# Transposing the gated FFN values on VectorE instead of TensorE in three of the four FFNs of a two-layer decoder trunk

## The chip, the cores and the metric

The kernel runs on one core of one Trainium2 chip. The metric is the device time of one execution in microseconds (us): the median of three runs was 1585.8 us, and they lay between 1585.21 and 1585.86. One more execution was recorded by the hardware profiler; its time was 1585.53 us and its span (from the first recorded instruction to the last) 1583.4 us. All rows below come from that one.

The engines are named as in the profile: PE is TensorE's matmul, PEld its loading of stationary operands, DVE is VectorE, ACT is ScalarE, POOL is GpSimd, and SP is SyncE, which issues the weight transfers.

## The reference

Two layers over 256 tokens of width 1024. Each layer adds to the running state `h`, in this order: half of a first FFN, the sum of four gated token mixers, a cross attention on a memory of 256 rows, and half of a second FFN. So there are four FFNs in all. One of them is

```python
def swiglu(x, w_gate, w_up, w_down):
    return (jax.nn.silu(x @ w_gate) * (x @ w_up)) @ w_down

h = h + 0.5 * swiglu(rms_norm(h, ffn1_norm[l]), ffn1_w_gate[l], ffn1_w_up[l], ffn1_w_down[l])
```

with `w_gate` and `w_up` of 1024 x 2816 and `w_down` of 2816 x 1024, all float32.

## The kernel before, in words

**Tiling.** The tokens are two blocks (`b`) of 128. Every large matrix product goes through `linear`: the stationary operand is a 128 x 128 piece of the transposed activations, the moving operand 512 columns of weights, and the result has the tokens on partitions. Float32 is imitated by three products of two-part numbers: each operand is a high part and a low part, and high x high, low x high and high x low are summed in PSUM. So one 128-deep step of one token block is three matmuls of 128x512.

**Weights.** `plan` lists all weights in the order of use, in chunks of 128 x 2048 (four 128-deep steps of 512 columns, 1 MB). `fetch` issues the transfer of a chunk on SP's queue into `wr`, and for each half of it ACT copies the high part into `wh` (L350) and DVE subtracts to get the low part `wl` (L351). There are three buffers each of `wr`, `wh` and `wl`. A chunk feeds 24 matmuls: 12 for each token block, in the order high x high, low x high, high x low, so that `wl` is needed last.

**An FFN.** The 2816 hidden columns are 11 groups of 256. A group's moving operand holds 256 gate columns beside 256 up columns, so a group is two chunks (the depth is 1024) and 48 matmuls; groups 0 and 1 go together, their chunks taken in turn. When a token block of a group is complete, `evac` runs ACT's Silu on the gate half (L557) and DVE multiplies it with the up half (L558) into `toks`, tokens on partitions. The second product needs the hidden columns on partitions, so `hidden` turns them: four 128 x 128 transposes on PE (L547) into a PSUM bank `ht`, and then `split` makes the two parts of it in the tile `hid`, the high one by ACT (L364) and the low one by DVE (L365). All 11 `hid` tiles live until the second product has read them: two halves of 512 output columns, each 22 steps deep in six chunks (the last of them half a chunk).

**Order of the work.** PE's instructions run in the order in which the program writes them. The other engines' streams are put in order by a planner, which goes by the program's order and by estimated durations; on the chip every engine then runs its own stream strictly in order. Small chains of work are Python generators: a chain advances at a `tick`, and `yield n` means not before n steps later; a step is one token block of one chunk, 12 matmuls. `hidden` begins with `yield 2`, so PE's four transposes of a group stand one whole chunk after the group's end.

**Pools.** The tag `toks` has three buffers of 128 x 512; the tag `gate` has four, and outside the FFNs holds gates of the mixers and values of the cross attention. In the first FFN of the first layer DVE also builds the attention bias tables (L642, L644).

Of the kernel before, what the change touches and what calls it, by code (L numbers as in the profile page):

```python
# [19 lines left out]
P = 128  # L20
# [3 lines left out]
NB = S // P  # L24
KD = D // P
DFF = 2816
KF = DFF // P
# [125 lines left out]
def program(tc, a, out, upto="all"):  # L153
    nc = tc.nc
    act, dve, pool, pe = nc.scalar, nc.vector, nc.gpsimd, nc.tensor
# [20 lines left out]
    def bank(name):  # L176
        return aux.tile([P, 512], F32, tag="aux", name=name)

    def m4(name, dtype=F32):
        return mp.tile([P, 1024], dtype, tag="m", name=name)  # L180
# [7 lines left out]
    def f2(name, tag="f", bufs=5):  # L188
        return fp.tile([P, 512], F32, tag=tag, name=name, bufs=bufs)
# [9 lines left out]
    ident = cp.tile([P, P], F32, tag="ident", name="ident")  # L199
# [21 lines left out]
    def pcol(l, name, i=0, n=1):  # L221
        o = l * NPC + PO[name][0] + i
        return pcs[:, o:o + n]
# [18 lines left out]
    def advance(c):  # L242
        try:
            c[1] = next(c[0])
            c[2] = now
        except StopIteration:
            chains.remove(c)
# [6 lines left out]
    def start(gen):  # L254
        c = [gen, 0, now]
        chains.append(c)
        advance(c)
        return c

    def begin():  # L260
        nonlocal now
        now += 1

    def tick():
        for c in list(chains):
            if c in chains and ready(c):
                advance(c)

    def finish(c):
        while c in chains:  # L270
            assert isinstance(c[1], int) or all(e in events for e in c[1]), c[1]
            advance(c)
# [12 lines left out]
    def plan():  # L285
# [16 lines left out]
        for l in range(L):  # L302
            yield from ffn(l, "1")
            yield from chunks([win[l, G_QK], win[l, G_RV]], KD, 512)
            yield from chunks([win[l, G_RG]], KD, 512)
            yield from chunks([a["wmisc"][l]], KD, MISC)
            for g in (G_X0, G_X1):
                yield from chunks([win[l, g]], KD, 512, HELD)
            yield from chunks([win[l, G_Z]], KD, 512)
            yield from branch(l, 0)  # L310
            yield a["wmla"][l], 1536, 0
            for g in (G_DQ, G_DK):
                yield from chunks([win[l, g]], KD, 512, HELD)
            yield from chunks([win[l, G_DV]], KD, 512)
            for i in range(1, 4):
                yield from branch(l, i)
            yield from chunks([a["w_out"][l, c] for c in range(2)], KD, 512)
            for n in ("xa_wk", "xa_wq", "xa_wv"):
                for c in range(2):
                    yield from chunks([a[n][l, c]], KD, 512, 0 if n == "xa_wv" else HELD)  # L320
            yield from chunks([a["xa_wo"][l, c] for c in range(2)], KD, 512)
            yield from ffn(l, "2")
# [31 lines left out]
    def weights(n):  # L354
        for _ in range(AHEAD - len(fetched)):
            fetch()
        hi, lo, m = fetched.pop(0)
        assert m == n
        return hi, lo


    def split(hi, lo, src):

        act.activation(hi, src, AF.Copy)  # L364
        dve.tensor_tensor(lo, src, hi.bitcast(F32), ALU.subtract)  # L365

    def linear(kt, n, xT, evacs):

        ps = [[lin.tile([P, 512], F32, tag="lin", name="lin") for _ in range(NB)] for _ in evacs]
        per = 2048 // n  # L370
        for k0 in range(0, kt, per):
            m = min(per, kt - k0)
            for p_, evac in zip(ps, evacs):
                hi, lo = weights(m * n)
                if now < 4:

                    begin()
                    for k in range(m):
                        for b in range(NB):
                            for part, w in ((0, hi), (1, hi), (0, lo)):  # L380
                                pe.matmul(p_[b][:, :n], lhsT=xT(part, k)[:, b * P:(b + 1) * P],  # L381
                                          rhs=w[:, k * n:(k + 1) * n], start=k == 0 and w is hi and part == 0, stop=False)
                    tick()
                    begin()
                    tick()
                    continue
                for b in range(NB):
                    begin()
                    for part, w in ((0, hi), (1, hi), (0, lo)):
                        for k in range(m):  # L390
                            first = k0 + k == 0 and w is hi and part == 0
                            last = k0 + k == kt - 1 and w is lo
                            pe.matmul(p_[b][:, :n], lhsT=xT(part, k0 + k)[:, b * P:(b + 1) * P],  # L393
                                      rhs=w[:, k * n:(k + 1) * n], start=first, stop=last)
                    if k0 + m == kt:
                        evac(b, p_[b][:, :n])
                    tick()
# [33 lines left out]
    def blk(b):  # L431
        return slice(b * P, (b + 1) * P)
# [91 lines left out]
    def norm(l, name):  # L524
        return Transposed(hh, pcol(l, name, 0, 8), "r" + name)

    def add_to_h(c, factor, nxt, wait=1):
        def evac(b, ps):
            nonlocal paced
            if factor == 1.0:  # L530
                paced = dve.tensor_tensor(h[b][c], ps, h[b][c], ALU.add)  # L531
            else:
                paced = dve.scalar_tensor_tensor(h[b][c], ps, factor, h[b][c], ALU.mult, ALU.add)
            if nxt is not None and b == NB - 1:
                nxt.begin(c, wait)
        return evac

    def ffn(xT, nxt):
        hid = {}

        def hidden(g, toks):
            yield 2
            t4 = m4("hid", F32R).rearrange("p (s f t) -> p s f t", s=2, f=2)
            ps = bank("ht").rearrange("p (f t) -> p f t", f=2)
            for b in range(NB):
                for k in range(2):
                    pe.transpose(ps[:, k, blk(b)], toks[:, b, k * P:(k + 1) * P], ident)  # L547
            split(t4[:, 0], t4[:, 1], ps)
            hid[g] = t4

        def group(g):
            toks = f2("toks", "toks", 3).rearrange("p (b t) -> p b t", b=2)

            def evac(b, ps):
                nonlocal paced
                sg = fp.tile([P, 256], F32, tag="sg", name="sg")
                act.activation(sg, ps[:, :256], AF.Silu, scale=xT.r[:, b:b + 1])  # L557
                paced = dve.scalar_tensor_tensor(toks[:, b], ps[:, 256:], xT.r[:, b:b + 1], sg, ALU.mult, ALU.mult)  # L558
                if b == NB - 1:
                    start(hidden(g, toks))  # L560

            return evac

        linear(KD, 512, xT, [group(0), group(1)])
        for g in range(2, 11):
            linear(KD, 512, xT, [group(g)])
        for c in range(2):
            linear(KF, 512, lambda part, k: hid[k // 2][:, part, k % 2, :], [add_to_h(c, 0.5, nxt, 1 if c else 5)])


    def tables():
# [671 lines left out]
    x = Given(hh, pcol(0, "ffn1", 0, 8), "rffn1")  # L1243
# [12 lines left out]
    made = start(tables())  # L1256
    for l in range(L):
        n = norm(l, "mix")
        ffn(x, n)
        if stages == 1:  # L1260
            break
        x = norm(l, "xa")
        mem, m = mixers(l, n, x)
        if stages == 2:
            break
        n = norm(l, "ffn2")
        cross(l, mem, m, x, n)
        if stages == 3:
            break
        x = norm(l + 1, "ffn1") if l + 1 < L else None  # L1270
        if x is None:
            fn = bias.rearrange("p h k -> p (h k)")[:, :D]
            act.dma_start(fn, a["fnorm"])
        ffn(n, x)
        if stages == 4:
            break
# [17 lines left out]
```

## Time and profile before

| | us |
|---|---|
| median of three runs | 1585.8 |
| profiled execution, its own time | 1585.53 |
| its span | 1583.4 |
| PE busy | 1572.2 |
| PEld busy | 1345.1 |
| DVE busy | 1065.2 |
| ACT busy | 830.2 |
| POOL busy | 26.0 |

Busy times are sums over the span. PE's matmuls are pipelined and their ends are modelled, so a duration of one matmul is longer than the distance from its start to the next one's; what a run of matmuls takes is read from the chain in order of time. In the chain (the work that ended last, followed back from the end) a line has the start, the length and the number of instructions. Where two DVE instructions stand as one line of the timeline, the length runs from the first's start to the last's end.

### The profile page before, as it was taken

The numbers are of one execution on the slowest core, as the hardware profiler recorded it, in microseconds if no ns is written. First come the engines' busy times: TensorE is split into PE (matmuls) and PEld (weight loads), VectorE is DVE, ScalarE is ACT, GpSimd is POOL, SyncE is SP. The second block draws the span as 40 slices with busy tenths as digits, with TensorE's granted clock in tenths as the row PEclk, the third lists the DMA queues.
The fourth block names the chain that finished last, engine by engine and source line by source line (L and its number), as shares of the span: only waits on it lengthen the run. The fifth ranks groups of instructions, "written<-read, shape, count | busy, mean of one in ns | idle before, by whom it ended". The sixth has DMA issues, their size and how long they took to land.

```text
span 1583.4 us, 20797 instructions
## 1 busy us (share of the span) xinstructions
PE 1572.2 (99%) x8208; PEld 1345.1 (85%) x8208; DVE 1065.2 (67%) x1704; ACT 830.2 (52%) x1236; POOL 26.0 (2%) x40
## 2 busy tenths in 40 slices
PE   9999999999999999999999999999999999999998
PEld 7888889898888988888888888898988899888886
DVE  5887699997787656554565546697656766565543
ACT  6744446566655545444454444475575555554443
POOL 0000000000000000000000000000000000000000
PEclk9999999999999999999999999999999999999999
DMA  7655544444655444555555556444546554455552
GB/s 291 239 180 179 194 169 160 165 164 144 212 214 177 169 160 163 187 182 182 191 188 188 183 176 209 151 159 157 184 149 237 186 186 164 156 182 176 191 174 74
DMA packets 43153, 284.73 MB, mean 180 GB/s; under 512 B 4784, under 2 KB 5168, under 8 KB 11056
## 3 DMA queue, kind: packets, MB, share of 16 engines
q1 hardware_dynamic: 40464, 276.12, 51.3%
q10 hardware_dynamic: 2592, 7.29, 1.4%
q8 instruction: 64, 1.05, 0.3%
q14 instruction: 33, 0.27, 0.0%
HBM read 282.34 MB, written 1.05 MB: 179 GB/s over the span
## 4 chain that ended last, share of the span: by engine, by line
PE 98%; DMA 1%; ACT 0%; DVE 0%; issue 0%; POOLq 0%; POOL 0%; ACTq 0%
PE lin L393 77%; PE lin L411 11%; PE tr L422 2%; PE ht L547 1%; PE xo L1191 1%; PE lin L381 1%; PE xs L1145 1%; DMA bcs<-bcols 1%; PE up L953 1%; PE my L869 0%; PE ds L1038 0%; PE ms L989 0%; PE pt L680 0%; DMA pcs<-pcols 0%; ACT wh L350 0%
## 5 line engine op out<-in xcount | busy, mean ns | idle before, releaser
L351 DVE TENSOR_TENSOR wl<-wr,wh 128x1024 fp32r<-128x1024 f32 (+3 forms) x536 | 624.7, 1191 | 375.1 <-ACT wh L350 372.7
L350 ACT ACTIVATE wh<-wr 128x1024 fp32r<-128x1024 f32 (+3 forms) x536 | 533.2, 1030 | 493.4 <-PE lin L393 381.7
L393 PE MATMUL lin<-wh,xh 128*128 128x512 f32 (+1 forms) x1200 | 328.5, 395 | 1.1 <-ACT wh L350 0.9
L393 PE MATMUL lin<-wl,xh 128*128 128x512 f32 (+1 forms) x1200 | 320.7, 389 | 0.6 <-DVE wl L351 0.6
L393 PE MATMUL lin<-wh,xl 128*128 128x512 f32 (+1 forms) x1200 | 320.4, 389 | 0.0
L393 PEld LDWEIGHTS lin<-wl,xh 128*128 128x128 f32 x1200 | 225.1, 188 | 48.0 <-DVE wl L351 1.4
L393 PEld LDWEIGHTS lin<-wh,xl 128*128 128x128 f32 x1200 | 225.3, 188 | 47.0
L393 PEld LDWEIGHTS lin<-wh,xh 128*128 128x128 f32 x1200 | 219.2, 188 | 43.7 <-ACT wh L350 2.2
L393 PE MATMUL lin<-wh,hid 128*128 128x512 f32 x704 | 176.0, 390 | 0.0
L393 PEld LDWEIGHTS lin<-wh,hid 128*128 128x128 f32 x704 | 131.6, 188 | 27.1
L393 PE MATMUL lin<-wl,hid 128*128 128x512 f32 x352 | 95.4, 389 | 0.0
L393 PEld LDWEIGHTS lin<-wl,hid 128*128 128x128 f32 x352 | 66.1, 188 | 13.9
L557 ACT ACTIVATE sg<-lin,rffn 128x256 f32<-128x256 f32 x88 | 40.9, 464 | 65.0 <-PE lin L393 63.7
L644 DVE SCALAR_TENSOR_TENSOR bias<-ge,d,bias 128x384 f32<-128x384 f32 x124 | 69.4, 610 | 0.3
L411 PE MATMUL lin<-xh,wh 128*128 128x256 f32 x384 | 62.0, 283 | 0.0
L558 DVE SCALAR_TENSOR_TENSOR toks<-lin,rffn,sg 128x256 f32<-128x256 f32 x88 | 42.3, 480 | 27.7 <-ACT sg L557 27.6
L411 PE MATMUL lin<-xh,wl 128*128 128x256 f32 x384 | 60.5, 279 | 0.0
L411 PE MATMUL lin<-xl,wh 128*128 128x256 f32 x384 | 60.5, 279 | 0.0
L411 PEld LDWEIGHTS lin<-xh,wh 128*128 128x128 f32 x384 | 52.0, 188 | 0.3
L411 PEld LDWEIGHTS lin<-xl,wh 128*128 128x128 f32 x384 | 51.7, 188 | 0.0
L411 PEld LDWEIGHTS lin<-xh,wl 128*128 128x128 f32 x384 | 51.7, 188 | 0.0
L444 ACT ACTIVATE junk<-h 128x512 bf16<-128x512 f32 x36 | 22.4, 623 | 30.6 <-DVE h L531 16.9
(395 smaller groups left out, 1559.4 us busy)
## 6 DMA issues: line engine op xcount, KB each, us to landing
wr<-gu SPq DMA_DIRECT2D x86, 1024.0 KB, 5.1
wr<-win SPq DMA_DIRECT2D x68, 1024.0 KB, 5.1
wr<-dn SPq DMA_DIRECT2D x40, 1024.0 KB, 4.9
wr<-wbr SPq DMA_DIRECT2D x16, 1024.0 KB, 4.9
wr<-w_out SPq DMA_DIRECT2D x8, 1024.0 KB, 5.2
wr<-xa_wk SPq DMA_DIRECT2D x8, 1024.0 KB, 4.9
wr<-xa_wq SPq DMA_DIRECT2D x8, 1024.0 KB, 4.9
wr<-xa_wv SPq DMA_DIRECT2D x8, 1024.0 KB, 5.0
```

Source lines behind the costliest of these rows:

```text
L350: last = act.activation(hi[:, s], r[:, s], AF.Copy)
L351: dve.tensor_tensor(lo[:, s], r[:, s], hi[:, s].bitcast(F32), ALU.subtract)
L381: pe.matmul(p_[b][:, :n], lhsT=xT(part, k)[:, b * P:(b + 1) * P], rhs=w[:, k * n:(k + 1) * n], start=k == 0 and w is hi and part == 0, sto ...
L393: pe.matmul(p_[b][:, :n], lhsT=xT(part, k0 + k)[:, b * P:(b + 1) * P], rhs=w[:, k * n:(k + 1) * n], start=first, stop=last)
L411: pe.matmul(ps[i][:, j * 256:(j + 1) * 256], lhsT=ws[w][:, o:o + P], rhs=xT(part, k0 + k), start=k0 + k + part + w + j == 0, stop=k0 + k = ...
L422: pe.transpose(ps[:, k * P:(k + 1) * P], src[:, k * P:(k + 1) * P], ident)
L444: act.activation(j[:, :src.free_size()], src, AF.Square, accum_out=out_)
L547: pe.transpose(ps[:, k, blk(b)], toks[:, b, k * P:(k + 1) * P], ident)
L557: act.activation(sg, ps[:, :256], AF.Silu, scale=xT.r[:, b:b + 1])
L558: paced = dve.scalar_tensor_tensor(toks[:, b], ps[:, 256:], xT.r[:, b:b + 1], sg, ALU.mult, ALU.mult)
L644: dve.scalar_tensor_tensor(bias[:, hd], ge, d8[:, hd, i + 1:i + 2], bias[:, hd], ALU.mult, ALU.add)
L953: pe.matmul(ps[:, :n], lhsT=lowT[p_][:, k0 + k, blk(b)], rhs=wm[w][:, o + k * n:o + (k + 1) * n], start=i == 0, stop=i == len(seq) - 1)
```

## The change

In all FFNs but the very first (`busy`), the PE transposes and their PSUM bank are gone. DVE transposes the same values from `toks` in SBUF into a tile `turned` in SBUF, with the tag `gate`. DVE's transpose turns blocks of 32 x 32. Each of the 16 instructions of a group takes one quarter of the partitions (32 tokens of each block) and four blocks of 32 hidden columns, 128 values for each of the 32 partitions, and writes them to the quarter of the partitions that these columns belong to. They go out in four batches of four, at four successive steps, and after the fourth comes the same `split`, which now reads SBUF. The second product asks for a group's tile through `hT`, which first drives a chain to its end if it has not come there yet.

```diff
-    def ffn(xT, nxt):
-        hid = {}
+    def ffn(xT, nxt, busy=False):
+        hid, started = {}, {}
 
         def hidden(g, toks):
-            yield 2
             t4 = m4("hid", F32R).rearrange("p (s f t) -> p s f t", s=2, f=2)
-            ps = bank("ht").rearrange("p (f t) -> p f t", f=2)
-            for b in range(NB):
-                for k in range(2):
-                    pe.transpose(ps[:, k, blk(b)], toks[:, b, k * P:(k + 1) * P], ident)
-            split(t4[:, 0], t4[:, 1], ps)
+            if busy:
+                yield 2
+                ps = bank("ht").rearrange("p (f t) -> p f t", f=2)
+                for b in range(NB):
+                    for k in range(2):
+                        pe.transpose(ps[:, k, blk(b)], toks[:, b, k * P:(k + 1) * P], ident)
+                split(t4[:, 0], t4[:, 1], ps)
+            else:
+
+                t = f2("turned", "gate", 4)
+                src = toks.rearrange("p b (k j a) -> p k b j a", k=2, j=4)
+                dst = t.rearrange("p (k b i a) -> p k b i a", k=2, b=2, i=4)
+                for i in range(4):
+                    for j in range(4):
+                        dve.transpose(dst[j * 32:(j + 1) * 32, :, :, i], src[i * 32:(i + 1) * 32, :, :, j])
+                    yield 1
+                split(t4[:, 0], t4[:, 1], t.rearrange("p (k t) -> p k t", k=2))
             hid[g] = t4
...
-                    start(hidden(g, toks))
+                    started[g] = start(hidden(g, toks))
...
+        def hT(part, k):
+            if k // 2 not in hid:
+                finish(started[k // 2])
+            return hid[k // 2][:, part, k % 2, :]
+
         for c in range(2):
-            linear(KF, 512, lambda part, k: hid[k // 2][:, part, k % 2, :], [add_to_h(c, 0.5, nxt, 1 if c else 5)])
+            linear(KF, 512, hT, [add_to_h(c, 0.5, nxt, 1 if c else 5)])
...
-        ffn(x, n)
+        ffn(x, n, l == 0)
```

The call for the second FFN of a layer, `ffn(n, x)`, is unchanged and so takes the new way in both layers.

## Rows read from the trace of the kernel before

**Rows 1.** The profile's page: busy time of each engine with its share of the span and its instructions, and the chain that ended last by engine and by line.

```profile
PE 1572.2 (99%) x8208; PEld 1345.1 (85%) x8208; DVE 1065.2 (67%) x1704; ACT 830.2 (52%) x1236; POOL 26.0 (2%) x40
...
PE 98%; DMA 1%; ACT 0%; DVE 0%; issue 0%; POOLq 0%; POOL 0%; ACTq 0%
```

**Rows 2.** The chain that ended last, in order of time, over the last FFN: start, length, what.

```profile
1418.71 0.44 PE ht L547 x4
1419.15 10.93 PE lin L393 x48
1430.08 0.44 PE ht L547 x4
1430.52 10.93 PE lin L393 x48
...
1509.65 0.44 PE ht L547 x4
1510.08 10.93 PE lin L393 x48
1521.01 0.44 PE ht L547 x4
1521.45 54.46 PE lin L393 x240
```

**Rows 3.** The same view in the second FFN of the first layer: the first and the last of nine neighbouring groups, and the second product behind them.

```profile
635.03 10.93 PE lin L393 x48
645.96 0.44 PE ht L547 x4
646.39 10.93 PE lin L393 x48
...
725.96 10.93 PE lin L393 x48
736.89 0.44 PE ht L547 x4
737.33 38.13 PE lin L393 x168
```

**Rows 4.** Busy time of each engine by stretch (ten groups of that FFN, and its second product), with the number of instructions; then the granted clock as a share of full speed, the DMA engines' busy share, and GB/s.

```profile
core 0: us, PE busy (x) PEld busy (x) DVE busy (x) ACT busy (x) POOL busy (x), PEclk, DMA share, GB/s
...
635.00:748.70 113.70, 113.70 (x520) 94.02 (x519) 61.26 (x69) 52.43 (x69) 0.00 (x0) 1.00 0.55 181
748.70:805.00 56.30, 56.30 (x258) 46.73 (x257) 31.26 (x37) 25.65 (x34) 1.07 (x1) 1.00 0.59 196
```

**Rows 5.** DVE's instructions in order of time over one group of that FFN; in brackets DVE's idle time before them and what ended it.

```profile
646.18 2.36 DVE L351 TENSOR_TENSOR wl<-wr,wh 128x1024 fp32r<-128x1024 f32 x2 [2.69 <-ACT wh L350]
648.45 0.68 DVE L365 TENSOR_TENSOR hid<-ht,hid 128x512 fp32r<-128x512 f32 x1
649.71 0.48 DVE L558 SCALAR_TENSOR_TENSOR toks<-lin,rffn,sg 128x256 f32<-128x256 f32 x1 [0.57 <-ACT sg L557]
652.10 1.23 DVE L351 TENSOR_TENSOR wl<-wr,wh 128x1024 fp32r<-128x1024 f32 x1 [1.91 <-ACT wh L350]
653.25 0.48 DVE L558 SCALAR_TENSOR_TENSOR toks<-lin,rffn,sg 128x256 f32<-128x256 f32 x1
653.64 1.22 DVE L351 TENSOR_TENSOR wl<-wr,wh 128x1024 fp32r<-128x1024 f32 x1
657.54 2.36 DVE L351 TENSOR_TENSOR wl<-wr,wh 128x1024 fp32r<-128x1024 f32 x2 [2.69 <-ACT wh L350]
```

**Rows 6.** DVE's rows by line and shape, over the whole span: count, busy time, mean ns of one, and its idle time before them.

```profile
L742 DVE TENSOR_SCALAR yr<-ro,mv,gnr 128x128 f32<-128x128 f32 x16 | 5.5, 404 | 4.6 <-POOL gnr L739 4.6
...
L632 DVE COPY bias<-cst 128x128 f32<-128x128 f32 x4 | 0.9, 219 | 3.8 <-DMA cst<-consts 3.8
...
L657 DVE TENSOR_TENSOR qc<-rp,rp 128x128 f32<-128x128 f32 x4 | 1.1, 285 | 0.0
...
L1050 DVE SCALAR_TENSOR_TENSOR dsb<-dsb,r 128x128 f32<-128x128 f32 x8 | 2.4, 346 | 0.0
...
L655 DVE TENSOR_TENSOR rp<-lin,tabr 128x256 f32<-128x256 f32 x4 | 1.7, 415 | 0.0
...
L558 DVE SCALAR_TENSOR_TENSOR toks<-lin,rffn,sg 128x256 f32<-128x256 f32 x88 | 42.3, 480 | 27.7 <-ACT sg L557 27.6
```

**Rows 7.** PE's matmuls in order of time at the start of a chunk, the second of the next group.

```profile
657.51 1.18 PE L393 MATMUL lin<-wh,xh 128*128 128x512 f32 x4
658.53 1.08 PE L393 MATMUL lin<-wh,xl 128*128 128x512 f32 x4
659.45 0.85 PE L393 MATMUL lin<-wl,xh 128*128 128x512 f32 x3
```

**Rows 8.** Who waited for whom from 635 to 748 us: total, times, the longest.

```profile
DVE wl L351 <- ACT wh L350: 46.9, 20, 3.0
ACT wh L350 <- PE lin L393: 46.5, 20, 3.4
ACT sg L557 <- PE lin L393: 14.6, 9, 1.6
DVE toks L558 <- ACT sg L557: 5.1, 9, 0.6
```

**Rows 9.** ACT's instructions in order of time over the same group.

```profile
645.08 2.01 ACT L350 ACTIVATE wh<-wr 128x1024 fp32r<-128x1024 f32 x2 [3.07 <-PE lin L393]
647.00 0.58 ACT L364 ACTIVATE hid<-ht 128x512 fp32r<-128x512 f32 x1
649.20 0.47 ACT L557 ACTIVATE sg<-lin,rffn 128x256 f32<-128x256 f32 x1 [1.62 <-PE lin L393]
651.01 1.06 ACT L350 ACTIVATE wh<-wr 128x1024 fp32r<-128x1024 f32 x1 [1.34 <-PE lin L393]
```

**Rows 10.** The page's DMA issues: the weight chunks of gate and up, KB each, median us from issue to landing.

```profile
wr<-gu SPq DMA_DIRECT2D x86, 1024.0 KB, 5.1
```

## The prediction

> **What bounds the kernel now.** I read the page first: PE is busy for 99% of the span and holds 98% of the chain that ended last [rows 1]. A busy PE need not be a PE at its pace, so next comes the chain in order of time. In an FFN it shows nothing but PE: 48 matmuls of a group, 0.44 us for the four transposes, the next 48, and no wait between [rows 2, 3]. Then the busy times by stretch say how near the other engines are: over ten groups DVE works 61.26 of 113.70 us and ACT 52.43, at a granted clock of 1.00, which is the 2.4 GHz level [rows 4]. The waits say why DVE idles there: for ACT's high parts, and ACT for PE to give a buffer back [rows 8]. Both are led by PE. So PE's instructions set the time of an FFN, and DVE has spare time, which the change spends.
>
> **What goes.** A group's pitch is (725.96 - 635.03) / 8 = 11.366 us [rows 3]. The same matmuls without transposes between run at 54.46 / 240 = 0.2269 us each [rows 2], and 38.13 / 168 gives the same [rows 3]; 48 of them are 10.89 us. So the transposes cost 11.366 - 10.89 = 0.474 us a group: 0.44 of their own and some 0.035 that the neighbouring matmuls lose at the two changes of kind. Three FFNs of 11 groups are 33 groups: 33 x 0.474 = 15.6 us, all on the path. Counting only the transposes' own time it is 33 x 0.44 = 14.5 us, the lower end of this term.
>
> **What comes.** 16 DVE transposes a group, 528 in all. The trace has none, so their price T is bounded by rows [rows 6]. One streams 128 values per partition. The cheapest instruction of that length is the copy at 0.219 us; the plain two-operand one takes 0.285, the one with a scalar besides 0.346; one that reads PSUM and two scalars (`yr`) takes 0.404. If a 4-byte value took two steps, it would cost like a row of 256: 0.415 or 0.480 us. I take 0.285, the row of a plain pass without a shortcut (the copy lies below it though it moves as much), and keep 0.219 and 0.480 as ends.
>
> DVE's load of a group is now 61.26 x 11.366 / 113.70 = 6.13 us [rows 4], and the new pitch 10.89 leaves 4.76. The transposes of groups 0 to 9 fall into the 9.5 pitches between the end of group 0 (half a pitch ahead of group 1's, since the two alternate) and the end of group 10; those of group 10 fall into the second product. So 160 T stands against 9.5 x 4.76 = 45.2 us. At 0.285 that is 45.6, and DVE ends 0.4 us late.
>
> Being late is free at first. The low parts that were done at 646.18 + 2.36 = 648.54 [rows 5] go with the chunk after next, as there are three buffers: that chunk starts at 657.51 and first reads them at 659.45 [rows 7]. This cover is 10.9 us now and 10.4 when a pitch has lost its 0.47. Only what DVE falls behind beyond 10.4 us stops PE. The full gain holds up to T = (45.2 + 10.4) / 160 = 0.348 us. Beyond that each FFN loses 160 T - 55.6, and at 15.6 / 3 = 5.2 us of loss the gain is used up: T = 60.8 / 160 = 0.380 us. What DVE has fallen behind it makes up in the second product, where it works 31.26 of 56.30 us [rows 4]. Group 10's tile is needed there last, behind five chunks of 24 matmuls, 27 us; 16 T and a split are 5 to 8 us.
>
> In rows 5 two equal instructions in a row take 2.36 us together where one takes 1.22, so the second starts 1.14 us behind the first: neighbours overlap by 0.08, and 16 that overlapped so would occupy 16 x (0.285 - 0.08) = 3.3 us instead of 4.6 [rows 5, 6]. The Trainium skill speaks against counting on that (VectorE: DVE Perf Modes, "Two Vector instructions with no wait between them"): an instruction whose output starts in another quadrant of partitions than the one before is held until all earlier ones have finished; all 16 change the quadrant they write, so by the rule they cost 4.6 us, and no row of this trace writes from one quadrant to another. The sum above has the full durations, so it stands either way. The same page ("The three transpose paths") gives 311 ns for VectorE on 128x128 in a 2-byte type; by it the sum would be 160 x 0.311 - 45.2 = 4.6 us late, under the cover, and no run here shows it.
>
> **What costs nothing.** ACT's and DVE's split read SBUF instead of PSUM and keep their length; ACT is busy for under half the stretch [rows 4]. The split runs two steps later than now, 5.4 us, with the second product further off than that except for group 10, treated above. `toks` is held for one group instead of half of one, with three buffers. `turned` takes buffers that the cross attention has left by then. The first FFN keeps its code. On SP nothing is moved, but chunks are asked for every 5.45 us instead of 5.68; one lands in 5.1 [rows 10].
>
> **The sum.** 1585.53 - 15.6 = 1569.9 us for the profiled execution, whose time is 0.27 below the median shown. From the median: 1570.2 us.
>
> **Rivals.**
>
> *DVE becomes the bound (slower).* Place: the gate and up products of the three FFNs. It decides from T = 0.380 us on, as worked out. At 0.415 DVE ends 66.4 - 45.2 = 21.2 us late, 10.8 beyond the cover; three times that, less 15.6, is +16.8: 1602 us. At 0.480 it is 3 x 21.2 - 15.6 = +48: 1634 us. For it: T has no row, and the room per instruction is 4.76 / 16 = 0.30 us, hardly over the 0.285 that I take. Against it: of the rows of 128 values only the one that reads PSUM passes 0.380, those from SBUF to SBUF lie under it [rows 6], and to reach it the values would have to go at half rate.
>
> *The wait moves into ACT's queue (little gain).* The high part of `hid` now waits for DVE instead of PE. In ACT's queue, which runs in order, the copies of the next chunk's high parts and the next Silu stand behind it, and DVE's subtraction waits for these. When DVE is the late one, ACT sits at that copy until the 16th transpose, and then DVE idles for the copy and a first half chunk: 0.58 + 1.06 = 1.64 us a group [rows 9]. Then DVE is 0.4 + 9.5 x 1.64 = 16.0 us late, 5.6 beyond the cover: 3 x 5.6 = 16.8 takes the 15.6 back, 1587 us. It needs over (10.4 - 0.4) / 9.5 = 1.05 us a group to cost anything; at 1.35 the result is 1579. For it: DVE's idle time today is just such hand-overs [rows 8]. Against it: the order is planned, three buffers lie between, and the copies for the chunk after next can stand ahead of `hid` in the queue, as they do now [rows 9].
>
> *The transfers set the pace (no change).* If 181 GB/s were all that the chunks could have, a pitch would stay where it is: 1586 us. Against it: the second product moves 196 GB/s without a wait on a transfer [rows 4].
>
> **How the numbers follow.** Full gain 0.67, the hand-overs 0.12, the slower DVE 0.17, the transfers 0.04. The likeliest gives 1570.2 us, and by its own bounds 1568.5 to 1574 (from somewhat more than 15.6 us, if a change of kind costs PE more than I saw, down to 11.8). The range reaches up through the hand-overs and the transfers to a DVE just past its break-even, 1592; what is left out is the slow end of the first rival, about 0.15. A difference under 0.2% (3.2 us) can't be told from no change. Faster: 0.67 and 0.10 of the hand-overs, 0.77. Same: 0.02 of them, the transfers, and 0.01 of a DVE at break-even, 0.07. Slower: the rest of that rival, 0.16.
>
> **What would show it.** After the change the chain should hold runs of `lin` without `ht` in the last three FFNs, at 0.227 us a matmul, the distance from one group to the next 10.89 us, and eleven `ht` groups should be left, all in the first FFN. DVE's row of transposes should have a mean of some 0.28 us and 528 entries; DVE's busy share of the gate and up stretches should rise from 54% to near 98%, with its waits for `wh` all but gone. If T is above 0.35, PE waits for `wl` in the later groups of each FFN and not in the first ones; if these waits are there with T below, the hand-overs are to blame and ACT shows long waits at the `hid` copy. The prediction is wrong if T passes 0.38 us, or if PE has waits at `wl` with DVE idle ahead of them.

## The result, and the profile after

The changed kernel takes 1569.63 us (median of four runs, 1569.23 to 1573.1) against 1585.83 us for the kernel before in the same runs: a ratio of 0.9904, with a 95% interval of 0.9886 to 0.9921. It is 16.2 us faster; 1570.2 us was forecast. The profiled execution took 1570.0 us, 15.5 us less than the one of before.

The page's first part shows what was removed and added: 132 fewer PE instructions, which are 33 groups of four, and 528 more on DVE, whose busy time grows by 152 us.

```profile
PE 1556.9 (99%) x8076; PEld 1332.9 (85%) x8076; DVE 1217.3 (78%) x2232; ACT 827.3 (53%) x1236; POOL 26.1 (2%) x40
```

The chain that ended last, in order of time, over the second FFN of the first layer and over the last FFN, answers to [rows 2, 3]: start, length, what.

```profile
610.19 160.53 PE lin L393 x708
770.73 0.87 PE tr L422 x8
...
1389.78 170.69 PE lin L393 x753
```

Where the chain had `ht` after every 48 matmuls, it now is one run of `lin` without a wait. 160.53 / 708 = 0.2267 us a matmul, so 48 take 10.88 us where a group's pitch was 11.366. That is 0.48 us a group and 16.0 us for 33 groups, as the 0.474 and 15.6 of the prediction.

The busy times over ten groups, to be held against [rows 4]: DVE rises from 54% of the stretch to 106.71 / 109 = 98%.

```profile
635.00:744.00 109.00, 109.00 (x482) 90.30 (x481) 106.71 (x224) 52.35 (x70) 0.00 (x0) 1.00 0.52 179
```

The new DVE row and the two of the split, by line and shape: the transpose takes 0.302 us. The high part from SBUF waits for the last transpose, and ACT idles 165 us for that in all.

```profile
L557 DVE STREAM_TRANSPOSE turned<-toks 32x128 f32<-32x128 f32 x528 | 159.6, 302 | 6.9
...
L364 ACT ACTIVATE hid<-turned 128x512 fp32r<-128x512 f32 x33 | 20.9, 633 | 164.8 <-DVE turned L557 164.8
```

DVE's instructions in order of time, over one group in the middle of that FFN, against [rows 5]:

```profile
657.93 5.04 DVE L557 STREAM_TRANSPOSE turned<-toks 32x128 f32<-32x128 f32 x16
663.00 1.23 DVE L351 TENSOR_TENSOR wl<-wr,wh 128x1024 fp32r<-128x1024 f32 x1
664.15 0.68 DVE L365 TENSOR_TENSOR hid<-turned,hid 128x512 fp32r<-128x512 f32 x1
664.75 1.22 DVE L351 TENSOR_TENSOR wl<-wr,wh 128x1024 fp32r<-128x1024 f32 x1
665.88 0.48 DVE L569 SCALAR_TENSOR_TENSOR toks<-lin,rffn,sg 128x256 f32<-128x256 f32 x1
666.28 1.21 DVE L351 TENSOR_TENSOR wl<-wr,wh 128x1024 fp32r<-128x1024 f32 x1
667.41 0.48 DVE L569 SCALAR_TENSOR_TENSOR toks<-lin,rffn,sg 128x256 f32<-128x256 f32 x1
667.80 1.21 DVE L351 TENSOR_TENSOR wl<-wr,wh 128x1024 fp32r<-128x1024 f32 x1
668.94 5.04 DVE L557 STREAM_TRANSPOSE turned<-toks 32x128 f32<-32x128 f32 x16
```

No bracket stands behind any line: DVE waits for nothing. Its own pitch is 668.94 - 657.93 = 11.01 us, a little longer than PE's 10.88, so it falls behind by 0.13 us a group. The 16 transposes stand in one block, with (5.04 - 0.30) / 15 = 0.316 us from one start to the next.

How near this is to the edge is read at the first groups. DVE's stream, and below it PE's matmuls on the same chunk:

```profile
626.78 1.24 DVE L557 STREAM_TRANSPOSE turned<-toks 32x128 f32<-32x128 f32 x4
628.06 0.48 DVE L569 SCALAR_TENSOR_TENSOR toks<-lin,rffn,sg 128x256 f32<-128x256 f32 x1
628.58 3.15 DVE L557 STREAM_TRANSPOSE turned<-toks 32x128 f32<-32x128 f32 x10
631.75 0.48 DVE L569 SCALAR_TENSOR_TENSOR toks<-lin,rffn,sg 128x256 f32<-128x256 f32 x1
632.27 3.17 DVE L557 STREAM_TRANSPOSE turned<-toks 32x128 f32<-32x128 f32 x10
635.46 0.69 DVE L365 TENSOR_TENSOR hid<-turned,hid 128x512 fp32r<-128x512 f32 x1
636.16 2.52 DVE L557 STREAM_TRANSPOSE turned<-toks 32x128 f32<-32x128 f32 x8
638.72 1.23 DVE L351 TENSOR_TENSOR wl<-wr,wh 128x1024 fp32r<-128x1024 f32 x1
639.86 0.68 DVE L365 TENSOR_TENSOR hid<-turned,hid 128x512 fp32r<-128x512 f32 x1
640.47 2.36 DVE L351 TENSOR_TENSOR wl<-wr,wh 128x1024 fp32r<-128x1024 f32 x2
```

```profile
640.00 1.07 PE L393 MATMUL lin<-wh,xh 128*128 128x512 f32 x4
640.91 1.07 PE L393 MATMUL lin<-wh,xl 128*128 128x512 f32 x4
641.82 1.07 PE L393 MATMUL lin<-wl,xh 128*128 128x512 f32 x4
```

Groups 0 and 1 end half a pitch apart, and the planner put the 32 transposes of both ahead of the next subtraction: for 12 us DVE makes no `wl`. The chunk that PE starts at 640.00 gets the second half of its low part at 640.47 + 1.22 = 641.69, and the third of the four matmuls from 641.82 on, at 642.27, reads it. 0.6 us are left of a cover that was 10.9 us before [rows 5, 7].

In the later groups the cover comes back only in part. PE's matmuls on two neighbouring chunks, to be held against DVE's rows from 663.00 on:

```profile
669.02 1.07 PE L393 MATMUL lin<-wl,xh 128*128 128x512 f32 x4
...
674.46 1.07 PE L393 MATMUL lin<-wl,xh 128*128 128x512 f32 x4
```

The half chunk behind a block of transposes is done at 664.75 + 1.22 = 665.97 and read by the third matmul from 669.02 on, at 669.47: 3.5 us later. The half ahead of the next block is done at 667.80 + 1.21 = 669.01 and read at 674.91: 5.9 us later. So a group's block takes 2.4 us of the cover for a while, and some 4.5 of the 10.4 us are missing even ahead of it: the first groups used them, and an engine whose pitch is longer than PE's does not win them back.

### The profile page after: what moved, and what is told of

It reads as the page before. It is cut to its first block, busy times and chain, and to the rows that moved or that the text cites. A ratio compares the mean times of both kernels' runs of the same rounds, so it can differ in the third digit from the quotient of the medians.

```text
span 1568.0 us, 21055 instructions
## 1 busy us (share of the span) xinstructions
PE 1556.9 (99%) x8076; PEld 1332.9 (85%) x8076; DVE 1217.3 (78%) x2232; ACT 827.3 (53%) x1236; POOL 26.1 (2%) x40
## 3 DMA queue, kind: packets, MB, share of 16 engines
q10 hardware_dynamic: 2592, 7.29, 1.4%
## 4 chain that ended last, share of the span: by engine, by line
PE 98%; DMA 1%; ACT 1%; issue 0%; DVE 0%; POOLq 0%; POOL 0%; ACTq 0%
PE lin L393 78%; PE lin L411 12%; PE tr L422 2%; PE xo L1208 1%; PE xs L1162 1%; PE lin L381 1%; PE up L970 1%; DMA cst<-consts 0%; PE my L886 0%; PE ds L1055 0%; ACT wh L350 0%; PE ms L1006 0%; DMA pcs<-pcols 0%; PE pt L697 0%; PE ht L548 0%
## 5 line engine op out<-in xcount | busy, mean ns | idle before, releaser
L393 PE MATMUL lin<-wh,xh 128*128 128x512 f32 (+1 forms) x1200 | 325.0, 392 | 0.8 <-ACT wh L350 0.7
L557 DVE STREAM_TRANSPOSE turned<-toks 32x128 f32<-32x128 f32 x528 | 159.6, 302 | 6.9
L364 ACT ACTIVATE hid<-turned 128x512 fp32r<-128x512 f32 x33 | 20.9, 633 | 164.8 <-DVE turned L557 164.8
L393 PEld LDWEIGHTS lin<-wl,hid 128*128 128x128 f32 x352 | 66.1, 188 | 13.7
```

Source lines behind the costliest of these rows:

```text
L557: dve.transpose(dst[j * 32:(j + 1) * 32, :, :, i], src[i * 32:(i + 1) * 32, :, :, j])
```

## The experiments

The theory that went into them is that of the prediction: PE alone sets the time of these FFNs, what its transposes cost is all gained, and DVE's are hidden in its room and in a cover of 10.4 us. The rivals: DVE at 98% already costs something; the gain has another source; the cover is shorter than thought.

**Neither transpose.** The loop of the 16 is replaced by a wait of four steps, and the split reads `toks`:

```diff
-                for i in range(4):
-                    for j in range(4):
-                        dve.transpose(dst[j * 32:(j + 1) * 32, :, :, i], src[i * 32:(i + 1) * 32, :, :, j])
-                    yield 1
-                split(t4[:, 0], t4[:, 1], t.rearrange("p (k t) -> p k t", k=2))
+                yield 4
+                split(t4[:, 0], t4[:, 1], toks)
```

> In the three FFNs nothing is transposed, neither by PE nor by DVE: the split reads the gated values as they stand, so the second product works on values in the wrong order; all else is as in the changed kernel. Theory (PE alone sets the time, and 15.6 us is what its transposes cost; DVE's 528 transposes are wholly hidden): the same time as the changed kernel, 1569.6 us within 2. Rival (DVE at nearly 100% costs part of the gain): faster than the changed kernel by more than 2 us.

Measured: 1569.1 us (ratio 0.9898, 0.9882 to 0.9915), 0.5 us from the changed kernel, inside the scatter of both. The busy times of the same stretch:

```profile
635.00:744.00 109.00, 109.00 (x482) 90.25 (x482) 60.83 (x69) 52.99 (x68) 0.00 (x0) 1.00 0.56 191
```

DVE is busy for 60.83 of 109 us and the time is the same: the 160 us of transposes on DVE cost nothing that can be measured.

**Both transposes.** PE's stay and are used; DVE's run beside them into a tile that is not read (`turn` holds the loop of the 16):

```diff
-            if busy:
+            if not busy:
+                start(turn(toks))
+            if True:
                 yield 2
                 ps = bank("ht").rearrange("p (f t) -> p f t", f=2)
```

> The other part alone: PE's transposes stay and feed the second product, and DVE's 528 transposes run besides into a tile that nobody reads. Theory: DVE's load of a group is 6.13 + 16 x 0.316 = 11.2 us against a pitch of 11.37, so the time of the kernel before, 1585.8 us within 2, and with PE's removal worth all of the 16.2 us. Rival (part of the gain comes from ACT and DVE reading SBUF or from the other order of their work): 2 us or more below 1585.8.

Measured: 1585.15 us against 1585.18 (ratio 1.0, 0.9991 to 1.001). DVE's 16 by themselves are worth nothing either way, with DVE busy for 107.87 of 113.70 us there. Taking away PE's four, and with them the split's reading of PSUM, is worth the whole gain. These two runs do not part the one from the other. The chain does: it holds PE alone in both kernels, and PE's 0.48 us a group make up 16.0 of the 16.2 us.

**The price of the quarters.** As the first, where the split reads `toks`, with transposes from the first quarter of the partitions to the first quarter:

```diff
-                        dve.transpose(dst[j * 32:(j + 1) * 32, :, :, i], src[i * 32:(i + 1) * 32, :, :, j])
+                        dve.transpose(dst[:32, :, :, i], src[:32, :, :, j])
```

> As the one without transposes, but with 16 DVE transposes a group of the same size that all read the first quarter of the partitions and write to the first quarter, into a tile that nobody reads. It measures the price of changing the quarter. If a change of the quarter makes each instruction wait for the end of the one before: the distance from one to the next falls from 0.316 us to some 0.2 us (duration less the overlap of 0.08 or more), the 16 take under 3.6 us, and the duration of one stays at 0.30. If the transposes never overlap: still 0.316 us and 5.0 us for 16. Time as the changed kernel, 1569.6 us, either way.

One group of it in DVE's order of time, and the tile's instructions with the shortest, median and longest duration in ns:

```profile
664.26 3.18 DVE L557 STREAM_TRANSPOSE turned<-toks 32x128 f32<-32x128 f32 x16
...
L557 DVE STREAM_TRANSPOSE turned<-toks x528: 256/256/293, 626.2 to 1505.9; 32x128 f32<-32x128 f32 x176
```

16 take 3.18 us instead of 5.04: (3.18 - 0.26) / 15 = 0.195 us from start to start instead of 0.316. The duration falls too, 0.256 for 0.302, which I had not expected. The change of quarter costs 0.12 us an instruction and 1.9 us a group, and within one quarter neighbours overlap. By the Trainium skill (VectorE: DVE Perf Modes, "Two Vector instructions with no wait between them") an instruction that reads or writes another quarter of the partitions than the last one did is held until all earlier ones have finished. The trace agrees with it: 0.316 us from start to start is more than the duration of 0.302, and 0.195 less than 0.256. The time of the one run, 1569.56 us, is that of the changed kernel.

**More transposes.** 18, 20 and 24 a group, by doing one in every second batch, one in each batch, or two in each batch twice (shown for 20):

```diff
-                    for j in range(4):
+                    for j in [*range(4), *range(1)]:
```

> 18 DVE transposes a group in the three FFNs instead of 16: one of each second batch is done twice, to the same place. At 0.316 us each DVE has 56.9 us of them against 45.2 us of room and ends 11.7 us late. Theory (a cover of 10.4 us comes first): 1.3 us lost in each FFN, 1573.5 us, or still 1569.6 if the cover is a little longer. Rival (no cover: whatever DVE has beyond PE's pitch stops PE): with the other 5.96 us of a group DVE needs 11.65 us where PE needs 10.89; 33 x 0.76 = 25 us over 1569.6, 1594 us.

> 20 DVE transposes a group: one of each batch is done twice. 63.1 us against 45.2 of room, 17.9 late. Theory: 7.5 us beyond the cover in each FFN, 1569.6 + 22.5 = 1592 us, with PE's waits at wl in the later groups of each FFN alone. Rival without cover: 33 x (12.28 - 10.89) = 46 us, 1615 us, with waits from the second or third group on.

> 24 DVE transposes a group: two of each batch are done twice. 75.7 us against 45.2, 30.5 late. Theory: 20.1 us beyond the cover in each FFN, 1569.6 + 60 = 1630 us. Rival without cover: 33 x (13.54 - 10.89) = 87 us, 1657 us. Rival (DVE never sets PE's time): 1569.6 us here and in the two with 18 and 20.

Measured: 1584.65 us with 18 (ratio 0.9996, 0.9986 to 1.0007), 1606.04 with 20 (1.0132, 1.0112 to 1.0152), 1662.15 with 24 (1.0486, 1.0465 to 1.0507). The theory's 1573.5, 1592 and 1630 are all too low; the rival without a cover has 1594, 1615 and 1657, too high for 18 and 20. With no cover at all, 33 groups of DVE's own pitch less 10.89 would be lost: the pitches in these traces are 11.69, 12.35 and 13.7 to 13.8 us, so 26, 48 and 92 to 96 us, and 15, 36 and 93 were lost. What is left as cover is (26 - 15) / 3 = 3.8 us an FFN with 18, some 4 with 20 and at most 1 with 24; not 10.4. With 24 a part of the loss may be PE's clock: between 640 and 770 us, where PE waits for `wl` for up to 3.4 us at a time, the granted clock is 0.93. With 18 the first wait is where the changed kernel had 0.6 us left, PE's timeline:

```profile
641.50 0.61 PE L393 MATMUL lin<-wl,xh 128*128 128x512 f32 x2
642.74 0.73 PE L393 MATMUL lin<-wl,xh 128*128 128x512 f32 x2 [0.62 <-DVE wl L351]
```

The block of the first two groups has four more transposes there, 1.3 us. Then the chain runs over PE for 35 us, and from 678 us on over DVE, the chain in order of time:

```profile
642.74 35.41 PE lin L393 x154
678.20 0.68 DVE hid L365
678.88 1.14 DVE wl L351
```

Behind each block of 18 the room shrinks by the 0.8 us by which DVE's pitch is longer than PE's, until PE's timeline has the next wait, at 703.44. DVE's row of a half chunk, PE's first row that reads it, and that wait:

```profile
690.48 1.22 DVE L351 TENSOR_TENSOR wl<-wr,wh 128x1024 fp32r<-128x1024 f32 x1
...
691.58 1.07 PE L393 MATMUL lin<-wl,xh 128*128 128x512 f32 x4
...
703.44 0.73 PE L393 MATMUL lin<-wl,xh 128*128 128x512 f32 x2 [0.37 <-DVE wl L351]
```

The half is done at 691.70 and read by the third matmul at 692.03: 0.3 us are left, where the changed kernel has some 3.5.

**The order of DVE's stream.** With 18, the weights asked for three chunks ahead in the program, so that the planner sees the subtractions first:

```diff
-AHEAD = 1
+AHEAD = 3
```

> 18 transposes a group as before, but the program asks for the weights three chunks ahead of their use instead of one, so that the planner's stream on DVE has a chunk's subtractions ahead of the transposes of the steps that come later in the program. DVE's work is the same, only its order changes. Theory (the cover is there, three buffers give it, and in the run with 18 the planner's order had used it up with the first two groups' 36 transposes in a row): at most 1.3 us lost in each FFN, 1569.6 to 1574 us, and no wait of PE for wl at the first groups. Rival (the cover is only some 3 us for another reason): 1584.7 us as with 18 before.

Measured: 1606.16 us (ratio 1.0131, 1.0117 to 1.0145), far off the theory's 1574 and worse than the same work in the other order. 4.2 of the 21.5 us by which it is slower than with 18 have nothing to do with DVE's transposes: the chain's run into the second FFN starts at 614.07 and not at 609.88. In the first FFN, whose transposes are PE's, DVE now has early subtractions ahead of the norm's sums that the gated values need, and PE waits for these values:

```profile
34.38 1.12 PE L548 MATMUL ht<-ident,toks 128*128 128x128 f32 x4 [5.37 <-DVE toks L569]
```

In the three FFNs one half is as expected: subtractions now stand between the transposes of groups 0 and 1, and the chain has no wait from 614.07 to 681 us, so PE ran 67 us without one. But DVE's pitch rises from 11.69 to 695.19 - 682.75 = 12.44 us. The timelines of ACT and, below it, DVE show why:

```profile
686.46 0.63 ACT L364 ACTIVATE hid<-turned 128x512 fp32r<-128x512 f32 x1 [7.29 <-DVE turned L557]
686.99 1.04 ACT L350 ACTIVATE wh<-wr 128x1024 fp32r<-128x1024 f32 x1
```

```profile
682.75 2.36 DVE L351 TENSOR_TENSOR wl<-wr,wh 128x1024 fp32r<-128x1024 f32 x2
...
687.12 0.69 DVE L365 TENSOR_TENSOR hid<-turned,hid 128x512 fp32r<-128x512 f32 x1 [0.18 <-ACT hid L364]
688.07 1.23 DVE L351 TENSOR_TENSOR wl<-wr,wh 128x1024 fp32r<-128x1024 f32 x1 [0.26 <-ACT wh L350]
...
695.19 2.36 DVE L351 TENSOR_TENSOR wl<-wr,wh 128x1024 fp32r<-128x1024 f32 x2
```

ACT stands at the copy of `hid` for 7.29 us until DVE has done its last transpose, with the next high part behind it, and then DVE, the late engine, idles 0.18 and 0.26 us for what ACT could not do. That is 0.44 of the 0.75 us; most of the rest is overlap that is lost because fewer of DVE's full-width instructions now stand next to each other. In the two groups before, where PE was not yet held, the two idle times are 0.70 and 0.25 us. In the changed kernel ACT waits too, for up to 5.9 us, but DVE has subtractions to do meanwhile whose high parts ACT had copied before, and waits for nothing. It is the mechanism of the prediction's second rival, 0.44 to 0.95 us a group here.

**The first FFN.** All eleven groups of it on DVE too; then five of them (2, 4, 6, 8 and 10), the others on PE:

```diff
-        ffn(x, n, l == 0)
+        ffn(x, n)
...
-            if busy:
+            if busy and g not in (2, 4, 6, 8, 10):
```

> The change in the first FFN too, where DVE also builds the bias tables. Theory (only what DVE falls behind beyond a cover of 10.4 us stops PE): DVE has 86.6 us of work in the 110.5 us of ten groups there, 105.8 without PE's transposes; 10 x 5.05 us more is 137, 31 us late, 21 beyond the cover, less 5.2 saved: 16 us slower than the changed kernel, 1585 us, less whatever of the bias work the planner can put off (down to 1575). Rival (DVE does not set PE's time in any FFN): 5.2 us faster, 1564 us.

> The changed kernel, and in the first FFN five of the eleven groups (2, 4, 6, 8 and 10) on DVE too, as far as its room and the cover go: 86.6 + 4 x 5.05 = 107 us of work in ten groups of 105.8 to 108 us, group 10's after them. Theory: not late beyond the cover, and 5 x 0.474 = 2.4 us of PE time saved: 1567.2 us. Rival (the bias work and the transposes get in each other's way as they do in all eleven): 1570 us or more.

Measured: 1583.98 us for all eleven (ratio 0.9994, 0.9984 to 1.0003), 14.4 us slower than the changed kernel, where 16 were expected. Ten groups of that FFN, and PE's wait for the low parts up to 190 us (total, times, the longest):

```profile
18.50:129.00 110.50, 100.95 (x415) 80.23 (x414) 104.54 (x253) 60.10 (x91) 2.13 (x3) 0.95 0.53 185
...
PE lin L393 <- DVE wl L351: 9.4, 7, 2.3
```

DVE is busy for 104.54 us of the 110.5 there, and PE waits for its low parts. That wait is 9.4 us and not the 21 of the sum. The granted clock is 0.95, where the changed kernel has 1.00: PE, after waits of up to 2.3 us, was at its lower level of 1.2 GHz for some 11 us (an estimate: 0.05 x 110.5 / 0.5). How the 14.4 us are made up was not separated, and that they come near 16 does not show the cover right. For five: 1569.6 us (0.9904, 0.9887 to 0.992), no change where 2.4 us of gain were expected. Who waited for whom up to 190 us, in the run with five:

```profile
PEld ht L548 <- DVE toks L569: 2.7, 3, 1.4
PE ht L548 <- DVE toks L569: 1.9, 2, 1.2
```

The six groups that stay with PE are transposed two steps after their end, and their gated values now come late from a busy DVE. PE waits 1.9 us for them, a wait that the changed kernel does not have. My sum for this run had looked at `wl` alone.

**Two groups at a time.** 16 transposes of 256 values per partition for two groups. `toks` holds both groups side by side (in the buffers of the mixers' `mg`), `turned` both results, now in one buffer that the bias tables' `ge` uses too (n is twice the number of groups):

```diff
-                src = toks.rearrange("p b (k j a) -> p k b j a", k=2, j=4)
-                dst = t.rearrange("p (k b i a) -> p k b i a", k=2, b=2, i=4)
...
+            src = pair[:, :, :n * P].rearrange("p b (k j a) -> p k b j a", k=n, j=4)
+            dst = t.rearrange("p (k b i a) -> p k b i a", k=n, b=2, i=4)
```

> As the changed kernel, but in the three FFNs two groups are transposed together: 16 instructions of 256 values per partition for two groups instead of 32 of 128 (group 10 is alone). One takes 0.302 + 128 / 960 MHz-steps as between the rows of 128 and 256 values, 0.133 us more: 0.435, at a distance of 0.449, 7.2 us for two groups instead of 10.1. Theory (PE alone sets the time): the same time as the changed kernel, 1569.3 within 1.5, with DVE's busy share in the gate and up stretches down from 98% to about 88%. Rival (DVE at 98% still costs something): below 1568.

> The transposes by pairs in all four FFNs. In ten groups of the first FFN DVE has 86.6 + 37 = 124 us against 105.8: 18 late, 7.5 beyond the cover, less 5.2 saved: 2 us slower than by pairs in three, 1571.5 us. If the planner can put off bias work to later stages, down to 1564. If the cover theory does not hold in the first FFN, 1575 and more.

> The transposes by pairs of groups in all four FFNs, with the weights asked for three chunks ahead. If order was what cost the run by pairs in all four its cover: 18 us late in the first FFN against a cover of 10.4, less 5.2 saved, 1569.1 + 2.4 = 1571.5 us, and down to 1566 if more of the bias work is put off behind the subtractions. If not: 1575 us as before.

Measured by pairs in three FFNs: 1569.14 us (0.9897, 0.9882 to 0.9913). An instruction takes 0.436 us, as worked out, and DVE's work falls by 9 us in ten groups:

```profile
L560 DVE STREAM_TRANSPOSE turned<-toks 32x256 f32<-32x256 f32 x240 | 104.5, 436 | 3.1
...
635.00:744.00 109.00, 109.00 (x482) 90.25 (x482) 97.29 (x159) 52.60 (x69) 0.00 (x0) 1.00 0.51 180
```

The time is the changed kernel's within 0.5 us: again DVE's work is hidden. By pairs in all four FFNs: 1575.17 us (0.9937, 0.9923 to 0.9951), and with the weights asked for early 1574.21 us (0.9936, 0.9922 to 0.9949), where 1571.5 was expected for both. For whom PE waited up to 215 us, first without and then with the early weights:

```profile
PE lin L393 <- DVE wl L351: 7.8, 5, 2.7
```

```profile
PE lin L393 <- DVE toks L579: 5.2, 1, 5.2
PE lin L393 <- DVE wl L351: 1.9, 3, 1.3
```

Without them PE waits 7.8 us for low parts, near the 7.5 that the theory has. But the run is 6.0 us slower than by pairs in three FFNs, and not 2.4; a part of the rest is PE's clock, 0.98 over 18.5 to 129 us, and it was not separated. With the early weights 1.9 us of the 7.8 are left, but PE waits 5.2 us for the first gated values, as in the run with 18. So the order gave most of the low parts' waits back and cost nearly as much at another place; the total alone hides both. No version was found that is measurably faster than the changed kernel.

## Why the prediction was right

**What goes.** Right in place and size: 0.474 us a group was forecast, 0.48 is read from the chain, and 33 times that is all but 0.2 us of the gain. The runs with neither and with both transposes show that DVE's transposes add nothing to it and take nothing from it.

**What comes.** T was put at 0.285 us; it is 0.302 long and 0.316 from start to start. 128 more values cost 0.436 - 0.302 = 0.134 us, as between the rows of 128 and 256 values, so the doubled price of a 4-byte value did not come. In one quarter the transpose takes 0.256 us, under the row of a plain pass; the change of quarter, of which the rows of before show nothing, lifts it above. That 0.285 came so near is therefore luck in part. DVE's other work was mis-sized the other way: 11.01 - 16 x 0.316 = 5.95 us a group and not 6.13, as its instructions now stand back to back. So DVE needs 11.01 us a group, and not 10.69. Its busy share of 98% is the forecast one by luck: there it left 2% of idle time, and here DVE has none; the 2% are the gaps between transposes.

**Being late is free at first.** Right that DVE may need more than PE's pitch without costing time; wrong in how much. The prediction put the full gain up to T = 0.348 and its end at 0.380, which is 6.1 us of transposes a group. With 18, at 5.7 us a group, the gain is gone already. The term that was mis-sized is the cover: 10.4 us were set against a lateness that grows evenly over ten groups, and the traces show that DVE's order decides how much of it is there. The 32 transposes of the first two groups in a row use 10 of its 10.9 us at once. Behind the blocks of later groups 3.5 us are left, and the runs with 18 and 20 behave as if 4 us were there. With two more instructions a group the forecast would have fallen. That it stood with 0.6 us left at the first groups is luck: nothing in the sum looked at the order.

**What costs nothing.** It held, but for one thing that I had wrong without effect: ACT's copy reads SBUF in 0.633 us where it read PSUM in 0.577.

**The rivals.** A slower DVE did not come, though it lay nearer than I thought. The hand-overs came half: ACT waits 165 us in all for the last transposes, 5 us a group, and it costs nothing while DVE has other work that is ready. Where the order took that work away, in the run with 18 and early weights, it cost 0.44 to 0.95 us a group. The transfers did not come: the pitch fell to 10.88 us and PE never waited. The 179 GB/s of this stretch lie under the rival's 181, but without transposes the same stretch moved 191.

**What stays open.** An order that has neither the block at the start nor the hand-over was not tried: the one run that spread the transposes brought the hand-over instead, and a wait in the first FFN. How much of the loss with 24, and with all eleven groups of the first FFN, is PE's lower clock was not separated.

## What to carry to other kernels

Where one engine runs without a gap, look for work to take off it: here it was gained whole, and the engine that got it could be filled to the brim, DVE from 54% to 98% at no cost. The room on that engine is no mere sum over a stage. Look at the longest block that its stream puts ahead of what the bound engine needs next, and at what stands in the other queues behind the results of that block. Before such work is moved, price one instruction with the partitions that it really reads and writes.

## What the runs showed of the hardware

A DVE transpose of 32 partitions by 128 float32 values has 0.195 us from start to start when source and target stay in one quarter of the partitions, and 0.316 us when the target changes each time and the source every fourth time; its own duration goes from 0.256 to 0.302 us. 256 values with the same changes take 0.436 us. Four 128x128 blocks therefore cost DVE 5.04 us in 16 instructions, or 3.6 us a group when two groups go together, where PE spent 0.48 us on them.

Where PE waited for DVE for some 2 to 3 us at a time, its granted clock fell: to 0.93 over 640 to 770 us with 24 transposes a group (the longest wait 3.4 us), and to 0.95 over 18.5 to 129 us with all eleven groups of the first FFN on DVE (2.3 us). In the changed kernel it is 1.00 in both stretches.
